# Gates and branches of a token mixer as token-major products of 512 columns

## The chip, the cores and the metric

The kernel runs on one core of a Trainium2 chip. The metric is device time in microseconds (us), the median of several runs; a profiled execution, taken once with the hardware profiler on, gives the trace. The engines are TensorE (PE; its loads of standing operands are PEld), VectorE (DVE), ScalarE (ACT), GpSimd (POOL) and SyncE (SP), which issues the weight transfers. SBUF holds tiles, PSUM holds the banks (128 x 512 floats) into which TensorE accumulates.

## The reference

Two layers, each a half-step SwiGLU, a token mixer and a second half-step SwiGLU, on 256 tokens of 1024 channels in float32. The mixer is what changes:

```python
h = rms_norm(x, mix_pre_g[l])
z = h @ w_in[l]
q, k, v, u_s, v_s, g_a, g_b = jnp.split(z, IN_SPLIT_POINTS, axis=-1)
y_attn = sliding_window_attention(q, k, v, attn_sinks[l])
y_sgu = spatial_gating(gelu(u_s), gelu(v_s), sgu_ln_g[l], sgu_ln_b[l], sgu_w[l], sgu_b[l])
merged = (jax.nn.sigmoid(g_a) * (y_attn @ w_attn_branch[l])
          + jax.nn.sigmoid(g_b) * (y_sgu @ w_sgu_branch[l]))
x = x + rms_norm(merged @ w_out[l], mix_post_g[l])
```

q, u, both gates, both branches and the out-projection are each 256 x 1024 times 1024 x 1024.

## The kernel before

Every operand of a product is split into a high part, which the product's number format holds exactly, and a low remainder. A product is then three passes: high by high, high by low, low by high. A weight arrives in units of 512 KB (128 x 1024 floats). `Stream` moves them: a DMA into one of four `raw` tiles, a cast of the high part on ScalarE (L138), and the subtraction of the remainder on VectorE (`low`, L152), which also issues the load of a later unit into the raw tile it frees. Nine units fit into the ring of `wh` and `wl`; the stream runs up to seven units ahead of the product.

The mixer's middle (`Mix.middle`) runs six products of eight units each: u, q, the gate gb, the gating unit's branch sg, the gate ga, the attention's branch at. Each is *feature-major*: `feature_major` (L254) lets 128 x 128 blocks of weights stand and moves 256 tokens past them, 8 blocks x 3 passes = 24 matmuls of 256 columns, and leaves 128 channels of all tokens. Two units fill one PSUM bank. The inputs, normalised tokens (`xt` in the profile) and the branches' inputs (in the pool `m8`, `m` in the profile), lie channels on partitions, and so does the result, as the out-projection needs it.

One unit is one slot. Small work is put between the units by hand: `at((slot, part), fn)` runs a function before (part 0) or behind (part 1) a unit's matmuls, and a generator that yields n goes on n halves later. So each engine's order is written in the program and fixed before it runs. The attention's six blocks run this way over the slots of q, gb, sg and ga.

- Every gate and branch pair is evacuated to SBUF by ScalarE three halves after it ends (`to`, L829).
- `gates`, behind the first unit of at, takes the sigmoid of gb and ga on ScalarE (L872, 128 x 1024 each, four of them) and multiplies gb's with the gating unit's branch on GpSimd (L874, two of 128 x 1024).
- `merge`, for every two units of at: VectorE multiplies the bank with ga (L883), GpSimd adds the other branch (L884), a slot later ScalarE casts the high part of the merged block (L886), half a slot on VectorE subtracts the remainder (L888). TensorE takes no part.
- `project` (L403) is the out-projection, *token-major*: 128 tokens by 128 channels of the merged block stand, 512 columns of weights move; `passes` (L252) issues 3 matmuls for each tile of tokens and half of the columns, 12 a unit. Its banks hold 128 tokens by 512 channels. It reads the merged block channel by channel from its first unit on.

`transpose4` (L217) turns four 128 x 128 blocks into one bank on TensorE; the attention and the steps behind the projections use it.

Of the kernel before, what the change touches and what calls it, by code (L numbers as in the profile page):

```python
# [40 lines left out]
AHEAD = 7  # L41
# [22 lines left out]
def trunk(ctx: ExitStack, tc: tile.TileContext, a: dict, out: bass.AP):  # L64
    nc = tc.nc

    def pool(name, bufs, **kw):
        return ctx.enter_context(tc.tile_pool(name=name, bufs=bufs, **kw))
# [5 lines left out]
    m8 = pool("m8", 6)  # L74
    n8 = pool("n8", 2)
    t4 = pool("t4", 2)
    t2 = pool("t2", 6)
# [87 lines left out]
    st = Stream()  # L165
# [6 lines left out]
    def halves():  # L172
        return [slice(h * 512, (h + 1) * 512) for h in range(2)]
# [37 lines left out]
    def bank():  # L211
        return new(mm, [P, 512], "mm")

    def transpose4(src, c0):
        ps = bank().rearrange("p (a b) -> p a b", a=4)
        for k in range(4):
            nc.tensor.transpose(ps[:, k, :], src[:, (c0 + k) * P:(c0 + k + 1) * P], ident)  # L217
        return ps

    def rows_of(t):  # L220
        return slice(t * P, (t + 1) * P)
# [26 lines left out]
    def passes(o, sh, sl, wh, wl, which, start, stop):  # L248

        every = ((sh, wh), (sh, wl), (sl, wh))  # L250
        for i in which:
            nc.tensor.matmul(o, every[i][0], every[i][1], start=start and i == 0, stop=stop and i == 2)  # L252

    def feature_major(o, u, ah, al):  # L254

        wh, wl = st[u]
        for k in range(KD):
            ks = slice(k * P, (k + 1) * P)
            nc.tensor.matmul(o, wh[:, ks], ah[:, k, :], start=(k == 0), stop=False)  # L259
            nc.tensor.matmul(o, wh[:, ks], al[:, k, :], start=False, stop=False)  # L260
            nc.tensor.matmul(o, wl[:, ks], ah[:, k, :], start=False, stop=(k == KD - 1))  # L261
        st.done(u)

    def feature_pair(o, u, both):
# [379 lines left out]
    class Mix:  # L644
# [144 lines left out]
        def middle(self, xt, xth, xtl, turn1, early):  # L789
            todo = {}  # L790
            now = [0]

            def at(slot, fn):
                todo.setdefault(slot, []).append(fn)

            def go(gen, half):
                wait = next(gen, None)
                if wait is not None:
                    at(divmod(half + wait, 2), lambda: go(gen, half + wait))

            def pairs(units, ah, al, evac):

                for j in range(KD):
                    for fn in todo.pop((now[0], 0), ()):
                        fn()
                    if j % 2 == 0:
                        o = bank().rearrange("p (a b) -> p a b", a=2)
                    feature_major(o[:, j % 2, :], units[j], ah, al)
                    for fn in todo.pop((now[0], 1), ()):
                        fn()  # L810
                    if units is self.at:
                        st.upto(self.rows[-1] + 1, 1)
                    else:
                        st.upto(units[j] + 1 + AHEAD)
                    if j % 2:
                        half = 2 * now[0] + 3
                        at(divmod(half, 2), lambda j=j, o=o, half=half: go(evac(j - 1, o), half))
                    now[0] += 1
# [12 lines left out]

            pairs(self.u, xth, xtl, lambda j, o: to(self.ut, j, o, AF.Gelu))

            self.qs = new(m8, [P, KD, S], "m8", F32R), new(m8, [P, KD, S], "m8", F32R)
            self.yah, self.yal = new(m8, [P, KD, S], "m8", F32R), new(m8, [P, KD, S], "m8", F32R)

            def evac_q(j, o):
                js = slice(j, j + 2)  # L840
                own = [(self.qs[r], slice(r * HD, (r + 1) * HD), slice((1 - r) * HD, (2 - r) * HD)) for r in range(2)]
                for q, b, _ in own:
                    nc.scalar.mul(q[b, js, :], o[b], 0.125)
                yield 1
                for q, b, other in own:
                    nc.vector.scalar_tensor_tensor(out=q[other, js, :], in0=o[b], scalar=0.125,
                                                   in1=f(q[b, js, :]), op0=ALU.mult, op1=ALU.subtract)
# [12 lines left out]
            gb = new(n8, [P, KD, S], "n8")  # L860
            pairs(self.gb, xth, xtl, lambda j, o: to(gb, j, o))
            so = new(n8, [P, KD, S], "n8")
            pairs(self.sg, self.ysh, self.ysl, lambda j, o: to(so, j, o))
            ga = new(m8, [P, KD, S], "m8")
            pairs(self.ga, xth, xtl, lambda j, o: to(ga, j, o))


            def gates():
                for gt in (gb, ga):
                    for h in range(2):  # L870
                        hs = slice(h * 4, h * 4 + 4)
                        nc.scalar.activation(gt[:, hs, :], gt[:, hs, :], AF.Sigmoid)  # L872
                        if gt is gb:
                            nc.gpsimd.tensor_tensor(out=so[:, hs, :], in0=so[:, hs, :], in1=gb[:, hs, :],  # L874
                                                    op=ALU.mult)

            at((now[0], 1), gates)
            self.mh, self.ml = new(m8, [P, KD, S], "m8", F32R), new(m8, [P, KD, S], "m8", F32R)

            def merge(j, o):  # L880
                js = slice(j, j + 2)
                y = new(t2, [P, 2, S], "t2")
                nc.vector.tensor_tensor(out=y, in0=o, in1=ga[:, js, :], op=ALU.mult)  # L883
                nc.gpsimd.tensor_tensor(out=y, in0=y, in1=so[:, js, :], op=ALU.add)  # L884
                yield 2
                nc.scalar.copy(self.mh[:, js, :], y)  # L886
                yield 1
                nc.vector.tensor_tensor(out=self.ml[:, js, :], in0=y, in1=f(self.mh[:, js, :]), op=ALU.subtract)  # L888

            pairs(self.at, self.yah, self.yal, merge)  # L890

            def behind(c, part):

                for fn in todo.pop((now[0] + c, part), ()):
                    fn()

            return behind
# [78 lines left out]
    ps = [transpose4(xs[0], h * 4) for h in range(2)]  # L976
# [9 lines left out]
    ps = [transpose4(xs[1], h * 4) for h in range(2)]  # L986
# [123 lines left out]
```

## Time and profile before

| what | value |
|---|---|
| median of 3 runs | 1188.09 us (1187.77 to 1188.12) |
| profiled execution | 1190.44 us, of which its span is 1188.7 us |
| matmuls | 7031 |
| ACT busy | 678.4 us (57%) |
| DVE busy | 836.3 us (70%) |
| POOL busy | 60.0 us (5%) |
| DMA | 220.90 MB, mean 186 GB/s, q1 56.8% of 16 engines |

The page gives the share of busy time of each engine, then the chain of work that ended last, followed back from the last instruction. TensorE's matmuls overlap, so the sum of their durations says more than the time they take; the distance between two starts is what a matmul costs. In a row of the timeline the two first numbers are the start and the duration in us, and the bracket at its end is the engine's idle time just before, with what ended it. The granted clock is the share of TensorE's full clock that the throttle let through.

### The profile page before, as it was taken

The page shows a single profiled execution, that of the slowest core. Times are in us where ns is not written, and L with a number is a line of the kernel's source. Part 1 is how long each engine was busy: PE and PEld are TensorE (multiplying, and loading weights), DVE is VectorE, ACT ScalarE, POOL GpSimd, SP SyncE. Part 2 cuts the span into 40 slices and gives each one's busy share as a digit, 9 for nine tenths or more (in the row PEclk, how much of TensorE's full clock was granted, in tenths as well). Part 3 has the DMA queues.
Part 4 walks back from the last instruction along what each step waited for, and adds up shares of the span by engine and source line. Part 5 has one row for each costly group of instructions (what it writes and reads, how often), then busy time and mean ns, then how long its engine had stood idle before and what let it go on. Part 6 is the DMA issues. An engine that isn't in the chain of part 4 may idle for free.

```text
span 1188.7 us, 18407 instructions
## 1 busy us (share of the span) xinstructions
PE 1173.2 (99%) x7031; PEld 1044.6 (88%) x7031; DVE 836.3 (70%) x1423; ACT 678.4 (57%) x1143; POOL 60.0 (5%) x40
## 2 busy tenths in 40 slices
PE   8999999998999999999999999999999999999997
PEld 7888888998999888888888888889999998888886
DVE  6768748778685976666586666578878668676753
ACT  5656644547676555664455665455577664665541
POOL 0000000001112100000000000000011040000000
PEclk9999999999999999999999999999999999999999
DMA  7577673554456636657725767645644653565660
GB/s 248 179 247 227 229 245 134 193 196 142 127 154 202 210 107 213 207 183 263 227 95 179 235 202 238 216 154 178 201 139 140 192 193 129 178 199 198 197 204 36
DMA packets 61288, 220.90 MB, mean 186 GB/s; under 512 B 7056, under 2 KB 7056, under 8 KB 61200
## 3 DMA queue, kind: packets, MB, share of 16 engines
q1 hardware_dynamic: 60912, 219.46, 56.8%
q8 instruction: 55, 0.90, 0.3%
q14 instruction: 33, 0.27, 0.1%
q10 hardware_dynamic: 288, 0.27, 0.1%
HBM read 218.65 MB, written 1.05 MB: 185 GB/s over the span
## 4 chain that ended last, share of the span: by engine, by line
PE 92%; DVE 3%; DMA 3%; ACT 1%; issue 1%; SPq 0%; DVEq 0%; ACTq 0%
PE mm L272 34%; PE mm L252 33%; PE mm L259 7%; PE mm L260 7%; PE mm L261 7%; DMA raw<-in_w_in 2%; PE mm L217 1%; PE mm L756 1%; DVE wl L152 1%; PE mm L720 1%; PE mm L719 1%; DMA raw<-in_ffn_w 1%; PE mm L769 0%; PE mm L768 0%; ACT wh L138 0%
## 5 line engine op out<-in xcount | busy, mean ns | idle before, releaser
L152 DVE TENSOR_TENSOR wl<-raw,wh 128x1024 fp32r<-128x1024 f32 x372 | 455.6, 1250 | 117.5 <-ACT wh L138 116.1
L138 ACT CAST wh<-raw 128x1024 fp32r<-128x1024 f32 x372 | 383.0, 1050 | 177.3 <-DMA raw<-in_ffn_w 70.4
L272 PE MATMUL mm<-xt,wh 128*128 128x512 f32 x1152 | 290.7, 393 | 0.7 <-DVE xt L950 0.7
L252 PE MATMUL mm<-wh,m 128*128 128x512 f32 x832 | 258.4, 390 | 0.0
L272 PEld LDWEIGHTS mm<-xt,wh 128*128 128x128 f32 x1152 | 207.3, 189 | 38.6 <-DVE xt L950 1.2
L252 PEld LDWEIGHTS mm<-wh,m 128*128 128x128 f32 x832 | 156.2, 188 | 32.1
L272 PEld LDWEIGHTS mm<-xt,wl 128*128 128x128 f32 x1152 | 157.1, 190 | 11.3
L252 PE MATMUL mm<-wl,m 128*128 128x512 f32 x416 | 161.9, 389 | 0.0
L272 PE MATMUL mm<-xt,wl 128*128 128x256 f32 x1152 | 160.6, 282 | 0.0
L259 PE MATMUL mm<-xt,wh 128*128 128x256 f32 x512 | 146.8, 287 | 0.0
L261 PE MATMUL mm<-xt,wl 128*128 128x256 f32 x512 | 145.3, 284 | 0.0
L260 PE MATMUL mm<-xt,wh 128*128 128x256 f32 x512 | 145.3, 284 | 0.0
L634 DVE TENSOR_TENSOR t<-mm,t 128x256 f32<-128x256 f32 x144 | 60.6, 421 | 97.0 <-ACT t L633 97.0
L260 PEld LDWEIGHTS mm<-xt,wh 128*128 128x128 f32 x512 | 98.8, 193 | 0.2
L259 PEld LDWEIGHTS mm<-xt,wh 128*128 128x128 f32 x512 | 98.8, 193 | 0.2
L261 PEld LDWEIGHTS mm<-xt,wl 128*128 128x128 f32 x512 | 98.6, 193 | 0.0
L252 PEld LDWEIGHTS mm<-wl,m 128*128 128x128 f32 x416 | 78.1, 188 | 16.0
L633 ACT COPY t<-mm 128x256 f32<-128x256 f32 x144 | 52.9, 368 | 46.6 <-PE mm L272 46.5
L259 PE MATMUL mm<-m,wh 128*128 128x256 f32 x256 | 72.5, 283 | 0.0
L260 PE MATMUL mm<-m,wh 128*128 128x256 f32 x256 | 72.4, 283 | 0.0
L261 PE MATMUL mm<-m,wl 128*128 128x256 f32 x256 | 72.4, 283 | 0.0
L636 ACT ACTIVATE t<-t 128x256 f32<-128x256 f32 x72 | 30.1, 418 | 73.8 <-DVE t L634 73.8
(156 smaller groups left out, 1324.3 us busy)
## 6 DMA issues: line engine op xcount, KB each, us to landing
raw<-in_ffn_w SPq DMA_DIRECT2D x264, 512.0 KB, 4.5
raw<-in_w_in SPq DMA_DIRECT2D x84, 512.0 KB, 4.3
raw<-in_w_sgu_branch SPq DMA_DIRECT2D x16, 512.0 KB, 3.7
raw<-in_w_attn_branch SPq DMA_DIRECT2D x16, 512.0 KB, 4.3
raw<-in_w_out SPq DMA_DIRECT2D x16, 512.0 KB, 4.6
gain<-in_ffn_post_g SPq DMA_DIRECT2D x4, 512.0 KB, 6.5
gain<-in_ffn_pre_g SPq DMA_DIRECT2D x3, 512.0 KB, 7.4
x<-in_x SPq DMA_DIRECT2D x4, 256.0 KB, 4.3
```

The costliest lines, as they stand in the source:

```text
L138: nc.scalar.copy(h, self.raw[u])
L152: nc.vector.tensor_tensor(out=lo, in0=self.raw.pop(u), in1=f(h), op=ALU.subtract)
L217: nc.tensor.transpose(ps[:, k, :], src[:, (c0 + k) * P:(c0 + k + 1) * P], ident)
L252: nc.tensor.matmul(o, every[i][0], every[i][1], start=start and i == 0, stop=stop and i == 2)
L259: nc.tensor.matmul(o, wh[:, ks], ah[:, k, :], start=(k == 0), stop=False)
L260: nc.tensor.matmul(o, wh[:, ks], al[:, k, :], start=False, stop=False)
L261: nc.tensor.matmul(o, wl[:, ks], ah[:, k, :], start=False, stop=(k == KD - 1))
L272: nc.tensor.matmul(out_, w[:, k * P:(k + 1) * P], x, start=(i == 0), stop=(i == len(todo) - 1))
L633: nc.scalar.copy(y[:, half, :], o[half][:, S:2 * S])
L634: nc.vector.tensor_tensor(out=y[:, half, :], in0=o[half][:, 0:S], in1=y[:, half, :], op=ALU.add)
L636: nc.scalar.activation(y[:, 0, :], y[:, 0, :], AF.Silu)
L719: nc.tensor.matmul(s[r][:, i, :], q_, kth[:, g, 0:nk], start=True, stop=False)
```

## The change

Both gates (gb, ga) and both branches (sg, at) become token-major products like the out-projection's. `row_major` takes one unit, which now holds 512 columns of two blocks of 128 input channels (the weights are repacked for it outside the kernel, `by_half`), and issues 12 matmuls of 512 columns: 2 tiles of tokens x 2 blocks x 3 passes. Four units fill two banks, one for each tile of tokens. `quads` evacuates the two banks in the two halves behind the fourth unit. u and q stay as they were.

The sigmoids keep their place and size; the multiplication on GpSimd is four of 128 x 512 instead of two of 128 x 1024. `merge` now runs once for each half of the columns and each tile of tokens: VectorE's product and GpSimd's addition as before, then, three halves later, four transposes on TensorE (the block is tokens on partitions, and the out-projection needs channels), then ScalarE's cast and VectorE's remainder from the transposed bank.

```diff
+    def row_major(o, u, m, ah, al):
+        wh, wl = st[u]
+        for t in range(NT):
+            for i in range(2):
+                k, ws = 2 * m + i, slice(i * 512, (i + 1) * 512)
+                passes(o[t], ah[:, k, rows_of(t)], al[:, k, rows_of(t)], wh[:, ws], wl[:, ws], (0, 1, 2),
+                       k == 0, k == KD - 1)
         st.done(u)
...
+            def quads(units, ah, al, evac):
+                for j in range(KD):
+                    def product():
+                        if j % 4 == 0:
+                            o[:] = [bank() for _ in range(NT)]
+                        row_major(o, units[j], j % 4, ah, al)
+                        return units[j]
+
+                    if j % 4 == 0:
+                        o = [None] * NT
+                    beside(product)
+                    if j % 4 == 3:
+                        for t in range(NT):
+                            half = 2 * now[0] + t
+                            at(divmod(half, 2), lambda h=j // 4, t=t, o=o[t], half=half: go(evac(h, t, o), half))
...
-            gb = new(n8, [P, KD, S], "n8")
-            pairs(self.gb, xth, xtl, lambda j, o: to(gb, j, o))
...
+            def rows_to(dst, h, t, o):
+                nc.scalar.copy(dst[:, t, halves()[h]], o)
+                yield from ()
+
+            gb = new(n8, [P, NT, D], "n8")
+            quads(self.gb, xth, xtl, lambda h, t, o: rows_to(gb, h, t, o))
...
             def gates():
-                for gt in (gb, ga):
-                    for h in range(2):
-                        hs = slice(h * 4, h * 4 + 4)
-                        nc.scalar.activation(gt[:, hs, :], gt[:, hs, :], AF.Sigmoid)
-                        if gt is gb:
-                            nc.gpsimd.tensor_tensor(out=so[:, hs, :], in0=so[:, hs, :], in1=gb[:, hs, :],
-                                                    op=ALU.mult)
+                for b in halves():
+                    nc.scalar.activation(gb[:, :, b], gb[:, :, b], AF.Sigmoid)
+                    for t in range(NT):
+                        nc.gpsimd.tensor_tensor(out=so[:, t, b], in0=so[:, t, b], in1=gb[:, t, b], op=ALU.mult)
+                for b in halves():
+                    nc.scalar.activation(ga[:, :, b], ga[:, :, b], AF.Sigmoid)
...
-            def merge(j, o):
-                js = slice(j, j + 2)
-                y = new(t2, [P, 2, S], "t2")
-                nc.vector.tensor_tensor(out=y, in0=o, in1=ga[:, js, :], op=ALU.mult)
-                nc.gpsimd.tensor_tensor(out=y, in0=y, in1=so[:, js, :], op=ALU.add)
-                yield 2
-                nc.scalar.copy(self.mh[:, js, :], y)
-                yield 1
-                nc.vector.tensor_tensor(out=self.ml[:, js, :], in0=y, in1=f(self.mh[:, js, :]), op=ALU.subtract)
-
-            pairs(self.at, self.yah, self.yal, merge)
+            def merge(h, t, o):
+                b = halves()[h]
+                y = new(t2, [P, 512], "t2")
+                nc.vector.tensor_tensor(out=y, in0=o, in1=ga[:, t, b], op=ALU.mult)
+                nc.gpsimd.tensor_tensor(out=y, in0=y, in1=so[:, t, b], op=ALU.add)
+                yield 3
+                at_ = (slice(None), slice(h * 4, h * 4 + 4), rows_of(t))
+                ps = transpose4(y, 0)
+                nc.scalar.copy(self.mh[at_], ps)
+                yield 1
+                nc.vector.tensor_tensor(out=self.ml[at_], in0=ps, in1=f(self.mh[at_]), op=ALU.subtract)
+
+            quads(self.at, self.yah, self.yal, merge)
```

In the rows below a name is a tile with its number, and L is the line of the kernel that the row is from. On TensorE, the end of the sixth unit of at in layer 0, before (`wh_727`, `wl_728` are the sixth unit, `m8_498` and `m8_499` the attention's output; the first three rows are the last matmuls of the sixth unit, the two others the first of the seventh):

```order
L259 MATMUL mm_757_4168<-m8_498_2561,wh_727_3980 128x256
L260 MATMUL mm_757_4168<-m8_499_2562,wh_727_3980 128x256
L261 MATMUL mm_757_4168<-m8_498_2561,wl_728_3981 128x256
L259 MATMUL mm_765_4234<-m8_498_2561,wh_730_4010 128x256
L260 MATMUL mm_765_4234<-m8_499_2562,wh_730_4010 128x256
```

The same place on TensorE now (`t2_756` and `t2_759` are the merged rows of the first 512 columns, tile 0 and 1 of the tokens; `mm_757` and `mm_758` are the banks of the second 512):

```order
L252 MATMUL mm_758_3833<-wh_727_3703,m8_498_2561 128x512
L252 MATMUL mm_758_3833<-wl_728_3704,m8_498_2561 128x512
L252 MATMUL mm_758_3833<-wh_727_3703,m8_499_2562 128x512
L217 MATMUL mm_763_3867<-ident_1_99,t2_756_3829 128x128 x4
L217 MATMUL mm_767_3879<-ident_1_99,t2_759_3846 128x128 x4
L252 MATMUL mm_757_3832<-wh_730_3721,m8_498_2561 128x512
```

Between the sixth and the seventh unit stand eight transposes, which read the merged rows.

VectorE beside that stretch, before (`L152` are remainders of weights; `m8_745` and `n8_755` are units of the next SwiGLU, the others of the out-projection):

```order
L152 TENSOR_TENSOR wl_743_4087<-raw_732_4014,wh_742_4086 128x1024
L883 TENSOR_TENSOR t2_748_4122<-mm_735_4018,m8_692_3721 128x512
L152 TENSOR_TENSOR m8_745_4092<-raw_738_4054,m8_745_4092 128x1024
L152 TENSOR_TENSOR wl_750_4126<-raw_741_4060,wh_749_4125 128x1024
L152 TENSOR_TENSOR wl_753_4157<-raw_744_4090,wh_752_4156 128x1024
L888 TENSOR_TENSOR m8_734_4017<-t2_748_4122,m8_733_4016 128x512
L883 TENSOR_TENSOR t2_758_4193<-mm_747_4097,m8_692_3721 128x512
```

VectorE there now:

```order
L152 TENSOR_TENSOR wl_744_3778<-raw_732_3725,wh_743_3777 128x1024
L152 TENSOR_TENSOR m8_746_3783<-raw_739_3757,m8_746_3783 128x1024
L152 TENSOR_TENSOR wl_749_3801<-raw_742_3763,wh_748_3800 128x1024
L152 TENSOR_TENSOR wl_752_3819<-raw_745_3781,wh_751_3818 128x1024
L923 TENSOR_TENSOR t2_756_3829<-mm_735_3730,m8_692_3528 128x512
L923 TENSOR_TENSOR t2_759_3846<-mm_736_3731,m8_692_3528 128x512
L152 TENSOR_TENSOR n8_754_3824<-raw_747_3786,n8_754_3824 128x1024
```

The first product with the gate stood behind one remainder of the next group and now stands, twice in a row, behind the remainders of two more units of the out-projection (`wl_749`, `wl_752`) and one of the next SwiGLU.

More of the change, by code (lines that the diff above doesn't have):

```diff
@@ L261, in feature_major @@
             nc.tensor.matmul(o, wl[:, ks], ah[:, k, :], start=False, stop=(k == KD - 1))
+        st.done(u)
+    def row_major(o, u, m, ah, al):
[5 more added lines that the diff above has]
+                       k == 0, k == KD - 1)
         st.done(u)
@@ L799, in go, with beside @@
                     at(divmod(half + wait, 2), lambda: go(gen, half + wait))
+            def beside(product):
+                for fn in todo.pop((now[0], 0), ()):
+                    fn()
+                u = product()
+                for fn in todo.pop((now[0], 1), ()):
+                    fn()
+                if u in self.at:
+                    st.upto(self.rows[-1] + 1, 1)
+                else:
+                    st.upto(u + 1 + AHEAD)
+                now[0] += 1
             def pairs(units, ah, al, evac):
@@ L803, in pairs @@
                 for j in range(KD):
-                    for fn in todo.pop((now[0], 0), ()):
-                        fn()
-                    if j % 2 == 0:
[L807 to L814, printed above, removed]
@@ L815, in pairs @@
-                    if j % 2:
-                        half = 2 * now[0] + 3
-                        at(divmod(half, 2), lambda j=j, o=o, half=half: go(evac(j - 1, o), half))
-                    now[0] += 1
+                    def product():
+                        if j % 2 == 0:
+                            o[:] = [bank().rearrange("p (a b) -> p a b", a=2)]
+                        feature_major(o[0][:, j % 2, :], units[j], ah, al)
+                        return units[j]
+                    if j % 2 == 0:
+                        o = [None]
@@ new lines, in pairs, with product @@
+                    beside(product)
+                    if j % 2:
+                        half = 2 * now[0] + 1
+                        at(divmod(half, 2), lambda j=j, o=o[0], half=half: go(evac(j - 1, o), half))
+            def quads(units, ah, al, evac):
+                for j in range(KD):
+                    def product():
+                        if j % 4 == 0:
+                            o[:] = [bank() for _ in range(NT)]
+                        row_major(o, units[j], j % 4, ah, al)
+                        return units[j]
+                    if j % 4 == 0:
+                        o = [None] * NT
+                    beside(product)
+                    if j % 4 == 3:
+                        for t in range(NT):
+                            half = 2 * now[0] + t
+                            at(divmod(half, 2), lambda h=j // 4, t=t, o=o[t], half=half: go(evac(h, t, o), half))
@@ new lines, in middle @@
+            gb = new(n8, [P, NT, D], "n8")
+            quads(self.gb, xth, xtl, lambda h, t, o: rows_to(gb, h, t, o))
+            so = new(n8, [P, NT, D], "n8")
+            quads(self.sg, self.ysh, self.ysl, lambda h, t, o: rows_to(so, h, t, o))
+            ga = new(m8, [P, NT, D], "m8")
+            quads(self.ga, xth, xtl, lambda h, t, o: rows_to(ga, h, t, o))
+            def gates():
+                for b in halves():
[4 more added lines that the diff above has]
+                    nc.scalar.activation(ga[:, :, b], ga[:, :, b], AF.Sigmoid)
@@ L1075, in rows, with by_half @@
         return w.reshape(L, m, k, P, n).transpose(0, 1, 3, 2, 4).reshape(L, m, P, k * n)
+    def by_half(w):
+        return np.concatenate([rows(w[:, :, :512], 2), rows(w[:, :, 512:], 2)], axis=1)
     arrays = {"x": src["x"].reshape(S, D)}
@@ L1089 @@
     arrays["w_in"] = np.concatenate(
-        [rows(vs, 1), rows(np.concatenate([v, k], axis=2), 4), cols(q), cols(u), cols(ga), cols(gb)], axis=1)
-    arrays["w_attn_branch"] = cols(src["w_attn_branch"])
-    arrays["w_sgu_branch"] = cols(src["w_sgu_branch"])
+        [rows(vs, 1), rows(np.concatenate([v, k], axis=2), 4), cols(q), cols(u), by_half(ga), by_half(gb)], axis=1)
+    arrays["w_attn_branch"] = by_half(src["w_attn_branch"])
+    arrays["w_sgu_branch"] = by_half(src["w_sgu_branch"])
     arrays["w_out"] = rows(src["w_out"], 1)
```

4 lines of the change are left out of this document (removed).

## The prediction, made before the changed kernel was run

> **What bounds the kernel now.** First the page: busy shares, then the chain of work that ended last.
>
> ```profile
> PE 1173.2 (99%) x7031; PEld 1044.6 (88%) x7031; DVE 836.3 (70%) x1423; ACT 678.4 (57%) x1143; POOL 60.0 (5%) x40
> ...
> PE 92%; DVE 3%; DMA 3%; ACT 1%; issue 1%; SPq 0%; DVEq 0%; ACTq 0%
> ...
> L259 PE MATMUL mm<-xt,wh 128*128 128x256 f32 x512 | 146.8, 287 | 0.0
> ...
> L259 PE MATMUL mm<-m,wh 128*128 128x256 f32 x256 | 72.5, 283 | 0.0
> ```
>
> TensorE is busy 99% of the span and carries 92% of the chain. So the time is TensorE's issue rate plus the few places where it waits, and an edit counts only as far as it changes one of these two. The changed products are the whole second form (the gating unit's and the attention's branch read m) and half of the first (both gates; the products u and q keep the other half): 256 + 256 matmuls at each of L259, L260 and L261, 1536 narrow ones in all, 24 in each of 64 weight units, 32 units a layer.
>
> TensorE's waits, all told, and what follows the longest:
>
> ```profile
> PE mm L719 <- DVE m L846: 3.0, 2, 2.7
> PE mm L252 <- ACT m L138: 2.4, 2, 2.0
> ```
>
> None lies in the changed products: there it runs without a gap. Two questions remain: what the wide form's rate is, and whether the new transposes find their data.
>
> **Part 1, the rate.** The timeline of TensorE at the attention branch of layer 0 (columns: start, duration, what), and the chain's rows for wide matmuls of the form that the change uses (activations standing, 512 columns of weights moving):
>
> ```profile
> 366.72 0.28 PE L261 MATMUL mm<-xt,wl 128*128 128x256 f32 x1
> 366.84 0.28 PE L259 MATMUL mm<-m,wh 128*128 128x256 f32 x1
> 366.96 0.28 PE L260 MATMUL mm<-m,wh 128*128 128x256 f32 x1
> ...
> 389.88 0.40 PE L252 MATMUL mm<-wh,m 128*128 128x512 f32 x1
> ```
>
> ```profile
> 390.04 21.11 PE mm L252 x93
> 411.15 0.44 PE mm L217 x4
> ...
> 423.43 0.87 PE mm L217 x8
> ```
>
> Narrow: a start each 0.12 us (durations overlap, so starts count). 366.84 to 389.88 is 23.04 us for eight units, 2.88 a unit, 24 x 0.12. Wide: 21.11 / 93 = 0.227 us. A unit becomes 12 x 0.227 = 2.72 us and saves 0.156; 64 units save **10.0 us**.
>
> The Trainium skill, "TensorE: Matmul & The Clock Gate", section "Back-to-back issue gap", gives N / 2.4 + 2.5 ns for an isolated gap, 109 ns at 256 columns and 216 at 512. By it a unit would save 30 ns and the change 1.9 us, an estimate, and the sum below would end 8.1 us higher. The rows here show 120 and 227 ns, so by them the narrow form loses more than that rule grants, and the measurement decides.
>
> **Part 2, the transposes.** Each layer merges two column halves of two row tiles: 4 merged blocks, 4 transposes each, 32 in the program, in four places with 8 adjoining. Eight cost 0.87 us (the row above): 4 x 0.87 = **3.5 us** on TensorE, with no cover, since it is the bound. Net of both: -6.5 us.
>
> **Part 3, the new wait.** Before, nothing on TensorE waits for the merge until the out-projection. Now the first eight transposes stand right after the sixth unit of the attention branch, 6 x 2.72 = 16.3 us after its start. On the clock of before (start at 366.84) that is **383.2**. They need POOL's two additions, which need the two DVE products. When do these come? ScalarE, VectorE, GpSimd and the weight queue there, in before:
>
> ```profile
> 367.66 1.28 ACT L872 ACT_TABLE_LOAD   x1
> 368.95 2.01 ACT L872 ACTIVATE n<-n 128x1024 f32<-128x1024 f32 x2
> 370.86 1.99 ACT L872 ACTIVATE m<-m 128x1024 f32<-128x1024 f32 x2
> 372.76 2.93 ACT L138 CAST wh<-raw 128x1024 fp32r<-128x1024 f32 x3
> 375.59 1.04 ACT L138 CAST m<-raw 128x1024 fp32r<-128x1024 f32 x1
> 379.89 1.05 ACT L138 CAST wh<-raw 128x1024 fp32r<-128x1024 f32 x1 [3.26 <-DMA raw<-in_w_out]
> 381.27 0.62 ACT L886 CAST m<-t 128x512 fp32r<-128x512 f32 x1 [0.33 <-POOL t L884]
> 381.90 1.05 ACT L138 CAST wh<-raw 128x1024 fp32r<-128x1024 f32 x1
> ```
>
> ```profile
> 373.82 4.41 DVE L152 TENSOR_TENSOR wl<-raw,wh 128x1024 fp32r<-128x1024 f32 x3 [8.62 <-ACT wh L138]
> 378.26 0.69 DVE L883 TENSOR_TENSOR t<-mm,m 128x512 f32<-128x512 f32 x1
> 378.87 1.22 DVE L152 TENSOR_TENSOR m<-raw,m 128x1024 fp32r<-128x1024 f32 x1
> 380.97 1.35 DVE L152 TENSOR_TENSOR wl<-raw,wh 128x1024 fp32r<-128x1024 f32 x1 [0.89 <-ACT wh L138]
> 382.98 1.23 DVE L152 TENSOR_TENSOR wl<-raw,wh 128x1024 fp32r<-128x1024 f32 x1 [0.66 <-ACT wh L138]
> 384.12 0.69 DVE L888 TENSOR_TENSOR m<-t,m 128x512 fp32r<-128x512 f32 x1
> 384.72 0.68 DVE L883 TENSOR_TENSOR t<-mm,m 128x512 f32<-128x512 f32 x1
> ```
>
> ```profile
> 370.09 4.79 POOL L874 TENSOR_TENSOR n<-n,n 128x1024 f32<-128x1024 f32 x2 [26.64 <-ACT n L872]
> 379.10 2.14 POOL L884 TENSOR_TENSOR t<-t,n 128x512 f32<-128x512 f32 x1 [4.22 <-DVE t L883]
> ```
>
> ```profile
> 375.99 1.46 SPq L119 DMA_DIRECT2D raw<-in_w_out  x2
> ```
>
> The sigmoids hold ScalarE from 367.66 to 372.8, so VectorE idles 8.62 us and subtracts its first weight remainder (L152) at 373.82. Four raw tiles are in flight, so that remainder frees the tile into which the next out-projection units are loaded: issued at 375.99, cast at 379.89 after a 3.26 us wait for the DMA, and at 381.90. By the order of the changed kernel the two products (L923) stand on VectorE behind the remainders of exactly these two units; those at 380.97 and 382.98 here.
>
> From the same rows: without L886's 0.62 us ahead of it, the second cast ends at 382.0 (right behind the one of 379.89) to 382.95, its remainder (1.23 us) at 383.2 to 384.2, and the first product (0.69 us) at 383.9 to 384.9. An addition of GpSimd alone is worth about 1.2 us: L874 takes 4.79 for 4 x 512 columns, 1.2 for each 512. (The 2.14 at 379.10 contains 0.99 in which the remainder of 378.87 still ran, to 380.09.) So the first block is there at 385.1 to 386.1. The second comes 1.2 later if GpSimd goes on at once, 2.4 later if VectorE's next remainder (1.22 us) goes first: 386.3 to 388.5.
>
> TensorE should finish its first four transposes and go on at 383.2 + 0.44. It loses the second block's arrival, plus 0.1 for the hand-over, less 383.64: 2.8 to 5.0 us. One bound further below: VectorE's first three remainders took 4.41 us where three of 1.22 are 3.66, and GpSimd's multiplication ran beside the first until 370.09 + 4.79 = 374.88. It is now four instructions instead of two, and if the remainder slips between two of them, all that follows comes up to 0.75 us earlier: **2.05 to 5.0**. I take **3.9** a layer, the middle of 2.8 to 5.0. Layer 1 repeats it: its branch starts at 950.74, its first remainder comes 6.99 us later, as 373.82 is 6.98 after 366.84.
>
> ```profile
> 950.74 0.28 PE L259 MATMUL mm<-m,wh 128*128 128x256 f32 x1
> ```
>
> ```profile
> 957.73 4.40 DVE L152 TENSOR_TENSOR wl<-raw,wh 128x1024 fp32r<-128x1024 f32 x3 [8.62 <-ACT wh L138]
> ```
>
> Two layers: **+7.8 us**. Before, the same lateness (the product at 384.72 serves a pair of units that TensorE left 6 us earlier) was hidden by the units and the out-projection behind it.
>
> The Trainium skill, "SBUF — State Buffer", section "SBUF: two separate sides", says that VectorE reading two SBUF operands and GpSimd hold a shared port for a whole instruction. The three remainders in 4.41 us and the addition in 2.14, against 3.66 and 1.2, agree; by it the later arrival of the second block (388.5) is as likely as the earlier.
>
> **Part 4, the clock after the wait.** The one comparable gap of before, and the windows around it (columns: length, busy time of each engine with its count, granted clock of TensorE, DMA):
>
> ```profile
> 272.57 0.33 PE L719 MATMUL mm<-kth,m 128*128 128x128 f32 x1 [2.66 <-DVE m L846]
> ...
> 273.39 0.30 PE L719 MATMUL mm<-kth,m 128*128 128x128 f32 x1 [0.38 <-DVE m L846]
> ```
>
> ```profile
> 274.00:276.00 2.00, 2.00 (x11) 2.00 (x11) 2.00 (x2) 1.26 (x1) 0.00 (x0) 0.50 0.42 172
> 276.00:278.00 2.00, 2.00 (x14) 2.00 (x14) 1.97 (x14) 0.00 (x0) 0.00 (x0) 0.69 0.80 252
> ```
>
> 2.66 + 0.38 us idle were followed by half the clock: (1 - 0.50) x 2 + (1 - 0.69) x 2 = 1.6 us lost. The new wait has 2.0 to 3.0 us idle (385.1 to 386.1 less 383.2, and the hand-over), four transposes, and 0.8 to 2 us more: nearest to this row, so 1.6 a layer, **+3.2 us**; the other bound is 0.
>
> **What I cost at nothing.** The second half's transposes come after two units of the out-projection; its merge is past the sigmoid's hold-up and has 1.1 to 2.3 us in hand: its transposes stand two units (24 x 0.227 = 5.4 us) behind the last matmul that it needs, less a product (0.69), two additions (2.4) and at most one remainder ahead (1.22). If that cover went, it would cost as much as it were late, up to 1 us a layer. Two banks are now held over four units where one was held over two; the evacuations (0.6 us each, as many as before) lie on ScalarE as before, and the tightest place, an attention block's scores behind the first gate's evacuation, has 0 to 0.6 us in hand: up to 0.3 us a layer. A gain from these I exclude, since TensorE waits for nothing there now.
>
> **Sum.** -10.0 + 3.5 + 7.8 + 3.2 = **+4.5 us**. The profiled execution took 1190.44 us (span 1188.7 and 1.7 around it), so its like would take 1194.9. The median of the runs, 1188.09, lies 0.2% below it, and on that scale I forecast **1192.6 us**.
>
> **Rivals.**
> 1. *The clock stays up, or the wait is short.* Without half clock the sum is +1.3 (1189.4); with 2.05 us a layer besides, -2.4 (1185.7). For it: the wait is cut in two by transposes. Against: so was the 2.66. Beside it the same page of the Trainium skill, section "What's actually happening", puts the return to half clock after an idle window of about 3.4 us that runs freely; by that rule a wait of that size might escape. The gap of 3.04 us that was followed by 0.50 does not decide it.
> 2. *The merge is in time*, the other side: faster. If the two remainders ahead of L923 came 3.8 us earlier (from the middles above: first product by 380.6, blocks by 381.8 and 383.6), the transposes would follow the sixth unit without a wait and the clock would hold: -6.5, **1181.6**. The price goes over to this side once the wait and clock together are under 4.1 us for both layers. For it: the DMA's 3.26 us wait and GpSimd's lock are both of such a size and might go. Against: both would have to, in both layers.
> 3. *Heavier.* Bank waits and a late second half on top: up to 2.6 more than the forecast, 1195.2, and a little beyond.
> 4. *The wide form saves nothing* (a 512-column matmul costs two narrow ones, 0.24): the 10.0 us goes, **1202.6**. Against it stand 93 matmuls in 21.11 us. The skill's formula would give 1200.7.
>
> That the change might not do what it says is excluded by its order: the narrow matmuls of these products are gone and the wide ones stand there.
>
> **Chances.** Forecast case (wait of 2.8 to 5.0 with half clock, 1190.4 to 1194.8): 0.56. Rival 1 (1185.7 to 1190.4): 0.25. Rival 2: 0.13. Rival 3: 0.04; rival 4: 0.02. The range **1185.7 to 1196.0** takes in the first two and most of the third; some 0.17 is left out. A measurement here can tell about 0.2% (2.4 us: 1185.7 to 1190.5) from no change: faster 0.15, the same 0.25, slower 0.60.
>
> **What would show it.** Part 1: L252 rows of 0.227 us in the gates. Part 2: 32 more rows at L217, 0.44 for four. Part 3: a wait of TensorE at L217 for POOL's L924, two or four times, 6 to 10 us together, after the sixth unit. Part 4: windows at 0.5 of the clock just after. The prediction is wrong if that wait is under 2 us a layer, or if TensorE's waits show a bank or a weight that I hold to be covered.

## The result, and the profile after

The changed kernel takes **1193.87 us** (median of 6 runs, 1192.03 to 1195.93) against 1187.81 us before (6 runs): a ratio of 1.0060, 95% interval [1.0047, 1.0073], 6 us slower. The profiled execution took 1194.83 us, its span 1193.1. One of the six runs of `split4` below took 2367.34 us, twice as long as the others at full granted clock, and is left out of its median.

From the page of the changed kernel, the busy shares and the chain that ended last:

```profile
PE 1171.4 (98%) x6295; PEld 1009.9 (85%) x6295; DVE 837.8 (70%) x1423; ACT 679.1 (57%) x1143; POOL 57.1 (5%) x44
...
PE 93%; ACT 2%; DMA 2%; DVE 2%; issue 1%; POOL 0%; SPq 0%; DVEq 0%; ACTq 0%; POOLq 0%
```

736 matmuls fewer (1536 narrow ones gone, 768 wide ones and 32 transposes new), and TensorE still sets the time. Its waits (what waited for what: us in total, times, longest):

```profile
PE mm L217 <- POOL t L924: 9.0, 4, 3.2
PE mm L252 <- ACT m L138: 2.9, 1, 2.9
```

The first row is new. The timeline of TensorE in layer 0: the first matmul of the attention branch, and the end of its sixth unit:

```profile
358.81 0.39 PE L252 MATMUL mm<-wh,m 128*128 128x512 f32 x1
...
374.90 0.39 PE L252 MATMUL mm<-wh,m 128*128 128x512 f32 x1
378.50 0.66 PE L217 MATMUL mm<-ident,t 128*128 128x128 f32 x4 [3.21 <-POOL t L924]
380.71 1.12 PE L217 MATMUL mm<-ident,t 128*128 128x128 f32 x4 [1.55 <-POOL t L924]
381.48 0.78 PE L252 MATMUL mm<-wh,m 128*128 128x512 f32 x1
382.05 0.63 PE L252 MATMUL mm<-wl,m 128*128 128x512 f32 x1
382.48 1.05 PE L252 MATMUL mm<-wh,m 128*128 128x512 f32 x2
```

It idles 3.21 us, turns the first block, idles 1.55 us, turns the second, and then starts wide matmuls 0.43 us apart (382.05 to 382.48) instead of 0.23. The windows there (length; busy time of TensorE, its weight loads, VectorE, ScalarE and GpSimd; granted clock; DMA) say why: the granted clock falls to 0.50, called half clock below; an unbroken stretch of it is called a spell.

```profile
376.00:378.00 2.00, 0.00 (x0) 0.00 (x0) 1.97 (x4) 1.39 (x2) 0.82 (x1) 1.00 0.81 270
378.00:380.00 2.00, 0.66 (x4) 0.42 (x4) 2.00 (x2) 0.81 (x2) 2.00 (x2) 0.93 0.61 229
380.00:382.00 2.00, 1.29 (x5) 1.25 (x6) 2.00 (x2) 0.86 (x2) 0.65 (x1) 0.50 0.59 203
382.00:384.00 2.00, 2.00 (x6) 1.57 (x5) 1.86 (x3) 1.39 (x2) 0.00 (x0) 0.50 0.65 190
384.00:386.00 2.00, 2.00 (x6) 1.52 (x6) 1.44 (x2) 0.00 (x0) 0.00 (x0) 0.50 0.58 186
386.00:388.00 2.00, 2.00 (x9) 1.65 (x8) 0.00 (x0) 1.05 (x1) 0.00 (x0) 0.86 0.88 330
```

What the merged rows waited for, on ScalarE, VectorE and GpSimd, one fence each. The branch starts at 358.81 here and at 366.84 in the rows of before, so 8.03 us are to be added to compare a time with those:

```profile
359.61 1.28 ACT L911 ACT_TABLE_LOAD   x1
360.91 2.01 ACT L911 ACTIVATE n<-n 128x1024 f32<-128x1024 f32 x2
362.82 1.99 ACT L915 ACTIVATE m<-m 128x1024 f32<-128x1024 f32 x2
...
371.76 1.05 ACT L138 CAST wh<-raw 128x1024 fp32r<-128x1024 f32 x1 [3.16 <-DMA raw<-in_w_out]
374.01 1.05 ACT L138 CAST wh<-raw 128x1024 fp32r<-128x1024 f32 x1 [1.20 <-DMA raw<-in_w_out]
```

```profile
365.78 4.68 DVE L152 TENSOR_TENSOR wl<-raw,wh 128x1024 fp32r<-128x1024 f32 x3 [9.31 <-ACT wh L138]
...
375.09 1.23 DVE L152 TENSOR_TENSOR wl<-raw,wh 128x1024 fp32r<-128x1024 f32 x1 [1.02 <-ACT wh L138]
376.35 1.29 DVE L923 TENSOR_TENSOR t<-mm,m 128x512 f32<-128x512 f32 x2
377.55 1.98 DVE L152 TENSOR_TENSOR n<-raw,n 128x1024 fp32r<-128x1024 f32 x1
```

```profile
377.18 3.47 POOL L924 TENSOR_TENSOR t<-t,n 128x512 f32<-128x512 f32 x2 [10.08 <-DVE t L923]
```

This is the chain that the prediction wrote down: sigmoids, late casts, two late loads, two remainders, the products, the additions. The second addition ended at 380.65, 3.47 us after the first began, with a remainder of VectorE (377.55) running beside it.

**The stages.** All runs below are read in the same way, by the distance in us between the first matmul of a product and the first of the next one. "at" is the attention's branch. "out" runs from the out-projection's first matmul to the first one of the next SwiGLU that reads a `wh` tile (24 matmuls of that SwiGLU, with weights kept elsewhere, come before it); "sum" also holds u and q (52.6 to 53.7 us in all runs but the first row).

| kernel, layer | gb | sg | ga | at | out | sum |
|---|---|---|---|---|---|---|
| before, 0 | 29.38 | 29.36 | 25.73 | 23.04 | 28.62 | 193.66 |
| before, 1 | 29.38 | 29.36 | 25.73 | 23.04 | 28.59 | 188.67 |
| changed, 0 | 28.21 | 28.20 | 24.47 | 30.59 | 29.45 | 193.63 |
| changed, 1 | 28.21 | 28.21 | 24.47 | 29.79 | 29.45 | 192.71 |

Three products are 1.2 to 1.3 us shorter each. The fourth is 7 us longer, where a saving of 1.3 should stand. Layer 0 of before has 5.0 us in its u and q that layer 1 lacks (57.5 against 52.6): TensorE's wait at L719 with its half clock.

### The profile page after: what moved, and what is told of

The parts are those of the page before. It is cut to its first block, busy times and chain, and to the rows that moved or that the text cites. A ratio compares the mean times of both kernels' runs of the same rounds, so it can differ in the third digit from the quotient of the medians.

```text
span 1193.1 us, 16939 instructions
## 1 busy us (share of the span) xinstructions
PE 1171.4 (98%) x6295; PEld 1009.9 (85%) x6295; DVE 837.8 (70%) x1423; ACT 679.1 (57%) x1143; POOL 57.1 (5%) x44
## 4 chain that ended last, share of the span: by engine, by line
PE 93%; ACT 2%; DMA 2%; DVE 2%; issue 1%; POOL 0%; SPq 0%; DVEq 0%; ACTq 0%; POOLq 0%
PE mm L252 46%; PE mm L282 34%; PE mm L259 3%; PE mm L260 3%; PE mm L261 3%; PE mm L217 1%; PE mm L766 1%; DMA raw<-in_w_out 1%; PE mm L730 1%; PE mm L729 1%; PE mm L699 1%; DVE wl L152 1%; ACT wh L138 1%; DMA raw<-in_ffn_w 1%; POOL t L924 0%
## 5 line engine op out<-in xcount | busy, mean ns | idle before, releaser
L152 DVE TENSOR_TENSOR wl<-raw,wh 128x1024 fp32r<-128x1024 f32 x372 | 454.6, 1248 | 111.7 <-ACT wh L138 110.0
L252 PE MATMUL mm<-wh,m 128*128 128x512 f32 x1088 | 343.5, 393 | 0.0
L282 PEld LDWEIGHTS mm<-xt,wh 128*128 128x128 f32 x1152 | 207.3, 189 | 38.3 <-DVE xt L992 1.2
L252 PE MATMUL mm<-wl,m 128*128 128x512 f32 x544 | 213.3, 392 | 0.0
L282 PEld LDWEIGHTS mm<-xt,wl 128*128 128x128 f32 x1152 | 157.2, 190 | 11.3
L282 PE MATMUL mm<-xt,wl 128*128 128x256 f32 x1152 | 160.6, 282 | 0.0
L252 PE MATMUL mm<-wh,xt 128*128 128x512 f32 (+1 forms) x480 | 144.1, 378 | 0.0
L252 PEld LDWEIGHTS mm<-wh,xt 128*128 128x128 f32 x480 | 88.4, 188 | 16.0
L252 PE MATMUL mm<-wl,xt 128*128 128x512 f32 (+1 forms) x240 | 87.5, 375 | 0.0
L259 PE MATMUL mm<-xt,wh 128*128 128x256 f32 x256 | 73.3, 286 | 0.0
L261 PE MATMUL mm<-xt,wl 128*128 128x256 f32 x256 | 72.4, 283 | 0.0
L260 PE MATMUL mm<-xt,wh 128*128 128x256 f32 x256 | 72.4, 283 | 0.0
L252 PE MATMUL mm<-m,xt 128*128 128x512 f32 x216 | 54.6, 397 | 0.0
```

The source lines that it names most:

```text
L152: nc.vector.tensor_tensor(out=lo, in0=self.raw.pop(u), in1=f(h), op=ALU.subtract)
L282: nc.tensor.matmul(out_, w[:, k * P:(k + 1) * P], x, start=(i == 0), stop=(i == len(todo) - 1))
```

## The experiments

The diffs are against the changed kernel unless another is named.

**Before, once more** (`before_again`).

> The kernel before, unchanged, profiled once more. In its first profile TensorE waited 2.66 and 0.38 us at L719 in layer 0 and ran 3.4 us at half clock behind it; from the first matmul of u to the first of the next SwiGLU layer 0 took 193.7 us and layer 1 188.7. Theory A (that wait comes and goes between executions, and the changed kernel's profile lacks it by chance): here the wait is absent or of another size, and a layer without it takes 188.7. Theory B (it belongs to the kernel before, and the change removed it): 3.0 us again, in layer 0 alone, and 193.7 there.

```profile
PE mm L252 <- ACT m L138: 2.1, 1, 2.1
...
PE mm L719 <- ACT m L843: 0.2, 1, 0.2
```

1187.43 us in its one run; the layers take 188.81 and 189.03 us. The wait for L846 is not there: theory A. So a usual layer of before takes 188.7 to 189.0 us, and the profile that the prediction was read from was a dear one, by 5.0 us.

**The changed kernel, once more** (`after_again`).

> The changed kernel again, beside the kernels below, for a second profile of its wait and clock. By its first profile: the attention branch takes 30.6 and 29.8 us in the two layers, TensorE waits 4.8 and 4.3 us at L217, and each wait is followed by 6.8 us of half clock; the time is 0.5 to 0.7% over the kernel before. If the half clock's length is a chance of where the idle time falls, a spell of 3.4 us may stand in its place, and the branch is then 1 to 1.5 us shorter.

```profile
PE mm L217 <- POOL t L924: 8.5, 4, 3.3
```

1194.02 us, a ratio to the kernel before of 1.0069 [1.0054, 1.0084]; branch 29.91 and 29.81 us, half clock for 6.83 us in both layers. The wait is the kernel's own, not one execution's.

**Transposes later** (`later`).

```diff
-                yield 3
+                yield 3 if h else 6
```

> The changed kernel with the first half's transposes three halves later (TensorE comes to them after the seventh and the eighth unit instead of the sixth), nothing else moved. Theory (TensorE waits for the merged rows, 4.5 us a layer, and pays 2.9 us a layer of half clock for it): the second block arrived 5.5 us after the end of the sixth unit, the eighth ends 5.45 us after it, so nearly all of the wait and the whole half clock go: 14 us less than the changed kernel, about 1180. Rival 1 (the wait is passed on: the out-projection now waits for ScalarE's cast and VectorE's remainder of the turned block, about 1.2 us or, behind a weight's cast and remainder, 3.5): 1182 to 1188. Rival 2 (the loss is the transposes and the wide form themselves): 1193, no change.

```profile
PE mm L252 <- DVE m L930: 1.5, 2, 0.8
...
PE mm L217 <- POOL t L924: 0.6, 1, 0.6
```

1184.80 us, 0.9987 [0.9977, 0.9996] of before. The branch takes 22.93 and 23.43 us, 7 us less, and no half clock stands in either layer. But "out" is now 31.1 us in both instead of 29.45: the out-projection waits for the remainder of the turned block. The theory and its first rival both hold, one for each part: the wait goes at the transposes, and 1.7 us a layer of it is passed on.

**The weight stream held** (`hold`).

```diff
                 if u in self.at:
-                    st.upto(self.rows[-1] + 1, 1)
+                    if u not in self.at[1:4]:
+                        st.upto(self.rows[-1] + 1, 1)
```

> The changed kernel with the weight stream held for three units (no cast and remainder is put behind the second, third and fourth unit of the attention's branch; they follow behind the fifth), so that VectorE's products L923 (here L924) stand behind one weight remainder after the sigmoids and not behind six; transposes where they were. Theory (the products are late because of what stands ahead of them on VectorE): they start some 9 us earlier, as soon as the banks and the sigmoid are there, TensorE's wait at the transposes is under 0.5 us, no half clock: about 1179 if the weights that come later still come in time. Rival (weights then come late for the out-projection or the next SwiGLU): TensorE waits there for ScalarE's or VectorE's split of weights, and part of it is lost again, 1182 to 1192.

```profile
PE mm L217 <- POOL t L925: 3.2, 3, 1.5
...
PE mm L252 <- DVE m L931: 0.9, 2, 0.6
PE mm L252 <- ACT m L929: 0.9, 1, 0.9
```

VectorE's first products, which now wait for TensorE's banks alone:

```profile
370.60 0.69 DVE L924 TENSOR_TENSOR t<-mm,m 128x512 f32<-128x512 f32 x1 [0.34 <-PE mm L252]
```

1187.16 us, 1.0004 [0.9995, 1.0013] of before. The branch falls to 22.65 and 23.68 us, so the products were late by what stood ahead of them on VectorE. The three waits at L217 are those of the second half's transposes, inside "out", which rises to 32.2 and 32.3: the casts and remainders that were held back come together and stand ahead of the second half's merge, whose first product starts 26.8 us into the branch against 23.0 in `split` below. The rival's price, though at the merge and not, as it said, at the weights themselves.

**The first gate's sigmoids ahead** (`split`).

```diff
+            def gate_b():
+                for b in halves():
+                    nc.scalar.activation(gb[:, :, b], gb[:, :, b], AF.Sigmoid)
+                    for t in range(NT):
+                        nc.gpsimd.tensor_tensor(out=so[:, t, b], in0=so[:, t, b], in1=gb[:, t, b], op=ALU.mult)
+
+            at((38, 1), gate_b)
             quads(self.ga, xth, xtl, lambda h, t, o: rows_to(ga, h, t, o))
...
-            def gates():
+            def gate_a():
                 for b in halves():
-                    nc.scalar.activation(gb[:, :, b], gb[:, :, b], AF.Sigmoid)
-                    for t in range(NT):
-                        nc.gpsimd.tensor_tensor(out=so[:, t, b], in0=so[:, t, b], in1=gb[:, t, b], op=ALU.mult)
-                for b in halves():
                     nc.scalar.activation(ga[:, :, b], ga[:, :, b], AF.Sigmoid)
```

> The changed kernel with the sigmoids of gb and GpSimd's multiplications moved three halves ahead, into ScalarE's idle time during the gate ga (its profile has 2.44 us and 0.77 us idle there); the sigmoids of ga stay. Theory (the hold-up begins with the 5.1 us that the sigmoids take of ScalarE): the casts begin 3.1 us earlier, the first three remainders no longer meet GpSimd's multiplication (4.68 us, against 3.66), so the products come some 4 us earlier; TensorE waits 0.5 to 1.5 us a layer and the clock stays up: 1193.9 - 2 x (3.5 + 2.9) = about 1181. Rival 1 (only the order on VectorE counts, DMA landings set it): the wait shrinks by under 1 us a layer and the half clock stays, 1192. Rival 2 (ScalarE has no room during ga): the attention branch's weights come late and TensorE waits in that product.

ScalarE, then TensorE and its waits:

```profile
359.29 2.01 ACT L919 ACTIVATE m<-m 128x1024 f32<-128x1024 f32 x2
361.20 2.94 ACT L138 CAST wh<-raw 128x1024 fp32r<-128x1024 f32 x3
```

```profile
374.94 0.60 PE L217 MATMUL mm<-ident,t 128*128 128x128 f32 x4
376.76 0.66 PE L217 MATMUL mm<-ident,t 128*128 128x128 f32 x4 [1.22 <-POOL t L928]
```

```profile
PE mm L217 <- POOL t L928: 1.6, 2, 1.2
```

1181.27 us, 0.9957 [0.9943, 0.9971] of before: as the theory said. The casts follow after 2 us of sigmoids instead of 5 us of table load and sigmoids, the first block is there in time, and only the second still comes 1.2 us late in layer 0 and 0.4 in layer 1. No half clock. The hold-up began at the sigmoids.

**The same, with the second block one unit later** (`split4`).

```diff
-                yield 3
+                yield 3 if h else 4
```

(beside the edit of `split`)

> The kernel with the sigmoids of gb moved ahead (split), and the second block's transposes one unit later in the first half (behind the seventh unit; the first block's stay behind the sixth). In split's profile TensorE waited 1.2 us in layer 0 and 0.4 in layer 1 there. Theory (only the second block was still late): both waits go, 1181.3 - 1.6 = about 1179.7, 0.6% under the kernel before. Rival (the out-projection then waits for the turned block, as in later): no gain over split, 1181 to 1182.

```profile
375.49 0.60 PE L217 MATMUL mm<-ident,t 128*128 128x128 f32 x4
...
378.71 0.60 PE L217 MATMUL mm<-ident,t 128*128 128x128 f32 x4
```

Neither row has a bracket: no wait. The branch takes 22.73 us and "out" 29.44 in both layers, and the median of its five other runs is **1179.98 us**, 0.9950 [0.9937, 0.9963] of before: faster than both kernels.

**The kernel before with the same sigmoids ahead** (`before_split`; the sigmoids of gb and their multiplications at slot 38 as in `split`, all else as before).

> The kernel before with only the sigmoids of gb and GpSimd's multiplications moved ahead, as in split; feature-major products as before, nothing turned. It tells whether the gain of split belongs to the change with its transposes or to the moved sigmoids themselves. Theory (before, nothing on TensorE waits for the merge until the out-projection, which is in time): no change, within 1 us of the kernel before. Rival (the moved sigmoids are worth something by themselves, whatever the products' form): 2 to 6 us less.

1185.96 us, 0.9997 [0.9987, 1.0007] of before, 23.04 and 28.57 us in at and out: no change. In the kernel before, where nothing on TensorE needs the merge early, the sigmoids' place is worth nothing.

**No transposes** (`noturn`, and `noturn_split` with the edits of `split4`). These kernels leave the turning out: the out-projection multiplies unturned rows of the same size, so its result is not the mixer's, but its matmuls are as many and as wide.

```diff
-                ps = transpose4(y, 0)
+                ps = y.rearrange("p (a b) -> p a b", a=4)
                 nc.scalar.copy(self.mh[at_], ps)
```

> The changed kernel without the transposes: the cast and the remainder take the merged rows unturned, so the out-projection gets wrong operands of the right size. TensorE then waits for the merge only at the out-projection, as in the kernel before. It prices the wide form alone. Theory (the wide form saves 0.156 us in each of 64 units): 10.0 us under the kernel before, 1176.5 against its 1186.5 in these runs, with no half clock in either layer. Rival (the wide form gains less here than in the out-projection, or the two banks held over four units cost time): 1178 to 1186.

`noturn` gave 1181.51 us, 0.9963 [0.9950, 0.9975] of before: 4.2 us less, not 10.

```profile
PE mm L252 <- DVE m L930: 2.5, 2, 1.5
```

The products took 28.21, 28.19, 24.47 and 21.76 us in both layers, what the theory gives, but "out" took 31.2 and 30.3 us. Was that a dearer out-projection, or the late merge again?

> split4 without the transposes (the out-projection takes unturned rows, wrong operands of the right size). noturn alone kept 4.3 us of TensorE's waits: in its profile the out-projection took 31.2 and 30.3 us instead of 28.6, and waited for VectorE's remainder L930. Theory (that is the same late merge, not a dearer wide form): with the sigmoids moved ahead the wait goes, the out-projection takes 28.6 us, each changed product is 1.2 to 1.3 us shorter than before, and the time is 9.7 us under the kernel before, about 1176.5, 3.5 us under split4. Rival (wide products make the out-projection slower): it still takes over 30 us, 1180.

1176.81 us, 0.9919 [0.9904, 0.9933]; the four products as in `noturn`, "out" 28.55 and 28.53 us. It was the late merge: even without the transposes the faster products reach the out-projection before the merge does.

**TensorE kept busy in its wait** (`fill`).

```diff
+                if h == 0:
+                    spare = bank()
+                    for _ in range(14 if t == 0 else 6):
+                        nc.tensor.matmul(spare, self.yah[:, 0, 0:P], flat(self.yah[:, 0:2, :]), start=True, stop=True)
                 ps = transpose4(y, 0)
```

> The changed kernel with TensorE kept busy in its wait: 14 and 6 more matmuls of 512 columns into a bank that nothing reads, ahead of the two first blocks' transposes of each layer (3.2 and 1.4 us at 0.227 each). The merged rows come when they came. Theory (of the loss, 2.9 us a layer is the half clock that follows the idle time): the windows stay at 1.0 and the time falls by 5.8 us though 40 matmuls more are issued, to about 1188. Rival 1 (the half clock has another cause than the idle time): it stays, 1193 to 1195. Rival 2 (the fillers only add to the path): up to 9.1 us more, 1203.

```profile
378.11 0.64 PE L217 MATMUL mm<-ident,t 128*128 128x128 f32 x4
380.32 0.65 PE L217 MATMUL mm<-ident,t 128*128 128x128 f32 x4 [0.18 <-POOL t L924]
```

```profile
376.00:388.00 12.00, 11.82 (x57) 9.39 (x56) 11.00 (x11) 6.25 (x7) 5.48 (x4) 1.00 0.75 235
961.00:973.00 12.00, 11.65 (x55) 9.14 (x54) 11.01 (x12) 6.52 (x8) 5.13 (x4) 1.00 0.68 218
```

1190.73 us, 1.0043 [1.0030, 1.0056] of before. The second transposes come 21.70 us after the branch's start, against 21.90 in the changed kernel, but the clock stays at 1.0 in both layers, and the branch takes 27.69 and 28.01 us instead of 30.59 and 29.79. With 40 more matmuls to do, the two branches are 4.7 us shorter together, and 4.0 against the second profile: the half clock follows the idle time, and is worth that. In all four runs the mean granted clock was 0.997 to 0.999, in the ten of the changed kernel 0.991 to 0.994. By the ratios to the kernel before the gain is 2 to 3 us, and the intervals overlap. The expected 5.8 is missed by about one because it took some lateness for clock: at full clock the branches are still 4.96 and 5.28 us longer than the 22.73 of `split4`, more than the 4.76 and 4.26 us of idle time in the changed kernel's list.

**The addition on VectorE** (`dveadd`).

```diff
-                nc.gpsimd.tensor_tensor(out=y, in0=y, in1=so[:, t, b], op=ALU.add)
+                nc.vector.tensor_tensor(out=y, in0=y, in1=so[:, t, b], op=ALU.add)
```

> The changed kernel with the merge's addition on VectorE (right behind its product) instead of GpSimd. In the changed kernel's profile the second addition took 2.25 us behind VectorE's next remainder, the first 0.51 on the chain. Theory (the second block is late by GpSimd's wait for VectorE's remainder): products and additions are four operations of about 0.65 us on VectorE, from 376.35 on, so the second block is there at about 379.0 instead of 380.7: 1.6 us less wait a layer, about 1190.6; and under 1186 if the clock stays up, since the idle stretch is then 2.6 us and not 3.2. Rival (the remainders behind are pushed 1.3 us later and TensorE waits for a weight): 1192 to 1194.

```profile
376.62 0.66 PE L217 MATMUL mm<-ident,t 128*128 128x128 f32 x4 [2.51 <-DVE t L924]
378.11 0.72 PE L217 MATMUL mm<-ident,t 128*128 128x128 f32 x4 [0.83 <-DVE t L924]
```

1191.01 us, 1.0037 [1.0027, 1.0048] of before. The waits are 6.2 us in all instead of 9.0, 1.4 us a layer less. GpSimd's turn behind VectorE's remainder is about 1.0 of that (the second addition of the changed kernel took 2.25 us, the first 1.26); the rest goes with the shorter addition, 0.69 us on VectorE. The clock does not stay up, but each spell of this profile is 3.41 us instead of 6.83. The profiled execution, 1188.02 us, is one of the two fastest of seven (the five others took 1190.13 to 1192.73), and the seven mean granted clocks, 0.992 to 0.996, suggest that spells were longer in some of the others.

## Why the prediction was right, and where it was short

It said 1192.6 us, in 1185.7 to 1196.0, slower with a chance of 0.60, by a new wait of TensorE for the merged rows. The measured 1193.87 is 1.3 us from it, and the place, the cause and the sign held. Its parts:

1. *Rate, -10.0 us.* The four products of a layer took 107.51 us before and 102.63 in `noturn_split`: -9.8 in two layers. Held. Rival 4, by which the wide form saves nothing, falls with it. By the formula of the Trainium skill ("TensorE: Matmul & The Clock Gate", section "Back-to-back issue gap") it would be 1.9 us, an estimate, and the measurement decides.
2. *Transposes, +3.5 us.* `split4` less `noturn_split`: 0.97 us in at and 0.90 in out, 3.7 in two layers. Held.
3. *The wait, +7.8 us, between 4.1 and 10.0.* The mechanism held link by link: moving the transposes (`later`), clearing VectorE ahead of the products (`hold`) and clearing ScalarE ahead of the casts (`split`) each took all or most of the wait away where it stood. The size was too small. What the prediction priced is the lateness of the second block, and `fill` shows it without the clock: 4.96 and 5.28 us, 10.2 in all, just past the upper bound. The idle time in TensorE's list, 9.0 us (4.76 and 4.26), is less, since the first block's transposes, 0.36 us from their start to the next matmul where nothing waits (375.49 in `split4`), run on in the record for 0.66 us and, at half clock in layer 1, for 1.11. Each link came at its late end. The early bound had the second cast right behind the one of 379.89, at 380.94; but the trace of before has that cast's weight landing at 381.82, so the rows left only the late bound, 381.90, and here the cast starts at 374.01, which is 382.04 on that clock. And the second addition took the later of the two turns.
4. *Half clock, +3.2 us.* Mis-sized too. The prediction priced it by the nearest row, a spell of 3.4 us. Here it lasted 6.83 us in both layers and both profiles, and cost what `fill` takes off the branches: 4.7 us, or 4.0 by the second profile. A part of each spell fell into the wait itself, where the clock cost nothing.
5. *Nothing for the second half and the banks.* Held: "out" grew by 0.83 to 0.86 us, its eight transposes, and no wait for a bank is in the list.

So the sum should have read -9.8 + 3.7 + 10.2 + 4.7 = +8.8 us, and not +4.5; the stages, against the second profile of before, give +8.5, and the two sessions' intervals 5.6 to 8.7 and 6.4 to 10.0. That the time itself was met so closely is partly luck: the prediction put +4.5 on the first median shown, 1188.09, and the kernel before took 1187.81 over six runs and 1185.7 to 1186.6 in later sessions. Between the two profiled executions the difference was 4.4 us, and not about 9, because before's held 5.0 us of a chance wait with its half clock.

Rival 1 fell with its reason, that a wait cut in two might keep the clock: `dveadd` has shorter waits, cut in the same way, and still half clock. Rival 2's time, 1181.6 us, is what the kernel takes when the merge is in time: `split` 1181.27, `split4` 1179.98. It named the price rightly; the two savings that it hoped for did not come by themselves, but an edit of the order brought the merge forward.

One thing the prediction did not see: it held the merge's lateness for hidden once it reached the out-projection. `noturn` shows that it was hidden only as long as the products were slow. With the wide form alone, 4.3 us of it came to light.

## What to carry to other kernels

A product's faster form also moves the time at which its consumer runs; ask of each result what is queued ahead of the work that makes it, on every engine in the chain, before a step on the bounding engine is made to need it. If it is late, look first for the earliest hold-up with idle room ahead of it (here 3 us of sigmoids and their table load on ScalarE), and not for a later place of the step that waits, which passes part of the wait on. A long wait of TensorE can cost its clock besides, so price it as wait and spell: here it did where TensorE idled 2.5 to 3.3 us and then 0.4 to 1.6 us more, and did not after the waits of up to 1.6 us in `split`, `later`, `hold` and `noturn`.

## What the hardware showed beyond what was expected

Until the last 6 us of a kernel, the half clock came in whole spells of 3.41 or 6.83 us. In the 3.41 us ahead of each spell within the mixer TensorE had been busy 0.36 to 1.06 us (0.86 before the one of before, 0.66 and 0.60 in the changed kernel, 1.06 and 0.93 in `dveadd`): a stretch need not be wholly idle. Spells ended after 3.41 us where it was busy 3.0 to 3.4 us of them (before, `dveadd`), and went on for as long again where it was busy 1.7 to 2.4 us (the changed kernel, four times). Layer 0 of the changed kernel, then of `dveadd`:

```profile
376.32:379.73 3.41, 0.66 (x4) 0.42 (x4) 3.38 (x4) 1.61 (x4) 2.55 (x2) 1.00 0.74 256
379.73:383.14 3.41, 2.43 (x8) 2.15 (x9) 3.27 (x4) 2.27 (x4) 0.92 (x1) 0.50 0.57 175
383.14:386.55 3.41, 3.41 (x9) 2.65 (x9) 2.30 (x3) 0.25 (x1) 0.00 (x0) 0.50 0.63 214
```

```profile
375.10:378.51 3.41, 1.06 (x9) 0.85 (x9) 3.20 (x5) 2.45 (x4) 0.00 (x0) 1.00 0.79 255
378.51:381.92 3.41, 3.41 (x11) 2.76 (x9) 3.41 (x5) 1.90 (x3) 0.00 (x0) 0.50 0.50 143
```

The Trainium skill, "TensorE: Matmul & The Clock Gate", section "What's actually happening", gives a window of 3413 ns, which agrees with the lengths; that about 1 us of work in it did not keep the clock up is what the runs add.

The two spells of the changed kernel start 587.09 us apart in both of its profiles, 172 times 3.413 us. Cut into windows of 3.413 us in step with the spells, the thirteen traces show one line between the two outcomes: of the windows at full clock, each with 1.61 us of work or more was followed by full clock (1.61 in `fill`, 1.69 in the changed kernel), and each with 1.48 us or less by half clock (1.48 in `hold`, 1.30 in `before_again`, both at the kernel's start). So what a wait costs in clock depends on where it falls among the windows: single waits of 2.89 us in the changed kernel and 3.05 us in `split4`, at the kernel's start, lay across two windows with 1.7 to 2.3 us of work in each, and the clock stayed up.
